# Weight blocks split into high and low halves by transfers instead of by engines, in a two-layer encoder trunk

## The chip, the cores and the metric

The kernel runs on one core of a Trainium2 chip. The metric is the device time of one execution, in microseconds (us). Profiles are of one execution, on the same core.

The engines are named as the profile names them: PE is TensorE (PEld its weight loads), DVE is VectorE, ACT is ScalarE, POOL is GpSimd, SP is SyncE. An engine works through its own instructions in order. A transfer is issued by one of these engines; its data then move by the 16 DMA engines.

## The reference

Two layers (DEPTH 2) of a bidirectional encoder over 512 tokens of width 1024, all in float32:

```python
x = layer_norm(x, ln_in_g, ln_in_b)
for l in range(2):
    proj = x @ w_in[l]                            # 1024 x 6816, split into q, k, v, latents, gates
    na_out  = neighbourhood_attention(...)        # 8 heads of 64, windows of 8 x 16 tokens
    df_out  = diff_attention(...)                 # 4 heads, two softmaxes each
    mla_out = latent_attention(...)               # 8 heads, low-rank q and kv, w_mla_qb, w_mla_kvb
    gates = sigmoid(gate_pre + b_gate[l])         # 3 x 1024 channels
    merged = sum of gates[b] * (branch_b @ w_branch[l, b])
    x = layer_norm(ALPHA * x + merged @ w_out[l])
    gu = x @ w_ffn_in[l]                          # 1024 x 5632
    x = layer_norm(ALPHA * x + (silu(gu[:, :2816]) * gu[:, 2816:]) @ w_ffn_out[l])
```

## The kernel before

PE multiplies in a reduced form of float32 (`float32r`). To keep float32 accuracy each operand is written as a high half (the value rounded to float32r) and a low half (what is left), and each product is made of three matmuls: high x high, high x low, low x high (`mm3`, lines 159 to 161). The activations lie in SBUF in halves as well (`xth`, `xtl` and the slots `r`).

Weights come in blocks of at most 128 x 1024 words. A block holds 2, 3 or 4 row tiles of 128 rows with 512, 336 or 256 columns. `wload` transfers a block from HBM into a tile `raw` (two buffers), issued by SP, and `wsplit` makes the halves: ACT copies `raw` into `whi` (line 141), DVE subtracts `whi` from `raw` into `wlo` (line 142). Both stand in a high-priority scope of the scheduler. `whi` and `wlo` have four buffers each, in rotation; a buffer is free when PE has done the last matmul that reads it. `wload_ks` calls `wload` for a whole product: 4 blocks of 2 x 512 for one half of the output projection (`out_proj`), 3 blocks for one half of one group of the FFN's second product (`ffn_down`), 3 + 3 + 2 row tiles for one half of the latents, two blocks for a gate or a pair of heads, one block for a merge of a branch.

Not by `wload` go the blocks of the first FFN product (`ffn_fast`: seven products of 24 matmuls with 256 columns each, whose blocks are sums and differences made on DVE and split by `wsplit`, in the same four buffers), the latent attention's own weights (`wload_flat`) and the first FFN step of a layer (`wload_slots`).

In a layer the order of the work is: the values of neighbourhood attention (`na_values`), `latents`, then the mixers (4 head pairs, 4 latent pairs, 4 differential heads) with the gates and merges placed between them by the table `PLAN`, then `out_proj`, and then the FFN, in which the halves of `ffn_down` for the group before stand between the steps of `ffn_fast`. The framework's scheduler sets each engine's order at build time from its own estimates of durations, so a change of one helper moves instructions throughout the program.

POOL does little: the small powers of the norms (`rpow`, lines 234 and 235) and a part of each layer norm.

## Time and profile before

| | |
|---|---|
| time, median of 2 runs | 1873.42 us (1872.22 to 1874.62) |
| the profiled execution's own time | 1868.85 us |
| its span, first to last instruction | 1867.1 us |
| PE busy | 1818.0 us, 11200 matmuls |
| DVE, ACT, POOL busy | 1324.6, 915.3, 134.9 us |
| data moved by DMA | 195.88 MB, mean 105 GB/s |

Times of rows are us from the span's start, or durations. A row of the groups gives line, engine, operation, out<-in, shapes, count, then busy us and mean ns of one, then how long the engine had been idle before these instructions and what ended that. A row of the timeline gives start, length, engine, line and operation, then the idle time before it and what ended it. PE's matmuls overlap in the records, so the pace of PE is the distance of their starts.

### The profile page before, as it was taken

Reading aid. Unit: us, or ns where it says so; the run is one execution under the profiler, and the core shown is the slowest. Engines: PE = TensorE matmul, PEld = TensorE weight load, DVE = VectorE, ACT = ScalarE, POOL = GpSimd, SP = SyncE. Lnnn points to the kernel's source line nnn. Section 1 sums busy time; section 2 is a strip of 40 time slices with the busy share of each in tenths; the row PEclk is TensorE's granted clock in tenths of the full one; section 3 lists DMA queues with packets and bytes.
Section 4 is the critical chain, followed back from the end, with each engine's and each line's share of the span. In section 5 each row is a group of like instructions: output and inputs, shape, how many; then the busy total and the mean of one; then the engine's idle time right before and its main releaser. Section 6 shows DMA issues by size and latency. Waiting matters only on the chain.

```text
span 1867.1 us, 28608 instructions
## 1 busy us (share of the span) xinstructions
PE 1818.0 (97%) x11200; PEld 1622.1 (87%) x11200; DVE 1324.6 (71%) x2198; ACT 915.3 (49%) x1629; POOL 134.9 (7%) x217
## 2 busy tenths in 40 slices
PE   7999999999999999999999999999999989999997
PEld 5988899988878999999779888999888789999995
DVE  6488887665568877777546888866655689776766
ACT  3567776555433443333236677755554245333330
POOL 4100000000004000000031000000000120000001
PEclk9999999999999999999999999999999999999999
DMA  7453232222261232323355432322233413323231
GB/s 255 115 163 94 89 91 85 74 85 74 91 212 37 78 115 89 115 89 104 105 156 156 123 97 86 91 62 86 74 101 120 158 46 103 112 91 113 91 102 68
DMA packets 167767, 195.88 MB, mean 105 GB/s; under 512 B 8528, under 2 KB 132688, under 8 KB 167632
## 3 DMA queue, kind: packets, MB, share of 16 engines
q1 hardware_dynamic: 167632, 194.05, 33.4%
q8 instruction: 88, 1.44, 0.3%
q14 instruction: 47, 0.39, 0.1%
HBM read 177.24 MB, written 9.44 MB: 100 GB/s over the span
## 4 chain that ended last, share of the span: by engine, by line
PE 87%; DVE 4%; DMA 3%; POOL 2%; ACT 2%; issue 1%; SPq 0%; POOLq 0%; DVEq 0%; ACTq 0%
PE acc L159 17%; PE acc L160 17%; PE acc L161 17%; PE sc L780 11%; PE pv L780 8%; DVE wlo L142 2%; PE tr L650 2%; PE pv L493 1%; DMA raw<-in_w_ffn_in_dram 1%; DMA f<-in_w_ffn_in_dram 1%; PE sc L479 1%; PE pv L658 1%; PE pv L657 1%; ACT whi L141 1%; PE sc L634 1%
## 5 line engine op out<-in xcount | busy, mean ns | idle before, releaser
L141 ACT ACTIVATE whi<-raw 128x1024 fp32r<-128x1024 f32 (+4 forms) x246 | 254.2, 1034 | 261.6 <-PE acc L160 49.4
L142 DVE TENSOR_TENSOR wlo<-raw,whi 128x1024 fp32r<-128x1024 f32 (+4 forms) x246 | 292.9, 1192 | 126.2 <-ACT whi L141 122.9
L159 PE MATMUL acc<-xth,whi 128*128 128x512 f32 x512 | 203.9, 398 | 0.2 <-ACT f L674 0.2
L161 PE MATMUL acc<-xth,wlo 128*128 128x512 f32 x512 | 202.7, 396 | 0.0
L160 PE MATMUL acc<-xtl,whi 128*128 128x512 f32 x512 | 202.6, 396 | 0.0
L159 PE MATMUL acc<-whi,r 128*128 128x512 f32 (+1 forms) x504 | 194.2, 392 | 4.3 <-DVE f L713 2.2
L141 ACT ACTIVATE whi<-f 128x1024 fp32r<-128x1024 f32 x100 | 104.7, 1056 | 188.8 <-PE acc L161 84.1
L161 PE MATMUL acc<-whi,r 128*128 128x512 f32 (+1 forms) x504 | 197.1, 391 | 0.0
L160 PE MATMUL acc<-wlo,r 128*128 128x512 f32 (+1 forms) x504 | 196.9, 391 | 0.0
L159 PE MATMUL acc<-whi,xth 128*128 128x256 f32 (+2 forms) x576 | 175.2, 306 | 3.0 <-ACT whi L141 2.2
L160 PE MATMUL acc<-wlo,xth 128*128 128x256 f32 (+2 forms) x576 | 175.6, 305 | 1.3 <-DVE wlo L142 1.3
L161 PE MATMUL acc<-whi,xtl 128*128 128x256 f32 (+2 forms) x576 | 175.8, 306 | 0.0
L780 PE MATMUL pv<-r,whi 128*128 128x256 f32 x960 | 173.9, 280 | 1.4 <-DVE P L848 1.4
L780 PEld LDWEIGHTS pv<-r,whi 128*128 128x128 f32 x960 | 148.0, 188 | 3.2 <-issue 2.1
L142 DVE TENSOR_TENSOR wlo<-f,whi 128x1024 fp32r<-128x1024 f32 x100 | 121.8, 1227 | 30.7 <-ACT whi L141 30.6
L780 PE MATMUL sc<-xth,whi 128*128 128x256 f32 x480 | 135.9, 283 | 0.0
L780 PE MATMUL sc<-xtl,whi 128*128 128x256 f32 x480 | 135.3, 282 | 0.0
L780 PE MATMUL sc<-xth,wlo 128*128 128x256 f32 x480 | 134.9, 282 | 0.0
L780 PE MATMUL pv<-r,wlo 128*128 128x256 f32 x480 | 134.0, 279 | 0.0
L234 POOL TENSOR_SCALAR ring<-ring 128x1 f32<-128x1 f32 x68 | 27.4, 404 | 1412.8 <-ACT otmp L499 811.1
L159 PEld LDWEIGHTS acc<-whi,r 128*128 128x128 f32 x504 | 94.2, 188 | 26.1 <-DVE f L713 3.1
L159 PEld LDWEIGHTS acc<-whi,xth 128*128 128x128 f32 x576 | 109.2, 190 | 8.0 <-ACT whi L141 2.9
(225 smaller groups left out, 4351.0 us busy)
## 6 DMA issues: line engine op xcount, KB each, us to landing
raw<-in_w_in_dram SPq DMA_DIRECT2D x64, 512.0 KB, 3.6
f<-in_w_ffn_in_dram SPq DMA_DIRECT2D x60, 512.0 KB, 3.5
raw<-in_w_ffn_out_dram SPq DMA_DIRECT2D x44, 512.0 KB, 3.6
raw<-in_w_in_dram SPq DMA_DIRECT2D x64, 256.0 KB, 3.3
raw<-in_w_ffn_in_dram SPq DMA_DIRECT2D x28, 512.0 KB, 3.6
raw<-in_w_branch_dram SPq DMA_DIRECT2D x24, 512.0 KB, 3.4
raw<-in_w_out_dram SPq DMA_DIRECT2D x16, 512.0 KB, 3.6
r<-r SPq DMA_DIRECT2D x56, 128.0 KB, 2.8
```

The lines of the kernel that those rows point to most:

```text
L141: A.activation(hi[:, :n], raw[:, :n], AF.Copy)
L142: V.tensor_sub(lo[:, :n], raw[:, :n], f32(hi[:, :n]))
L159: T.matmul(o, lh[0], rh[0], start=first, stop=False)
L160: T.matmul(o, lh[0], rh[1], start=False, stop=False)
L161: T.matmul(o, lh[1], rh[0], start=False, stop=last)
L234: G.tensor_scalar(dst, src, eps, None, op0=OP.add)
L479: T.matmul(sc, qs[j][:, tsl(t)], ks[j][1], start=False, stop=True)
L493: T.matmul(po[:, 0:256], ch_[:, tsl(k)], v, start=k == 0, stop=False)
L634: T.matmul(sc, q[0][:, tsl(t)], k[1], start=False, stop=False)
L650: T.transpose(pt[:, tsl(i)], prs[i % 2][:, tsl(kp + i // 2)], ident)
L657: T.matmul(oc, v, ph[:, c], start=kt == 0, stop=False)
L780: T.matmul(o[:, c], w[a][:, j, f], x[e], start=fresh and mi == 0 and j == 0 and n == 0, stop=j == 3 and n == 2, skip_group_check=True)
```

## The change

`wload` no longer uses `raw`, SP or DVE. POOL issues a transfer from HBM straight into `whi`; since the target is float32r and the source float32, it casts. ACT then writes the negated high half into `wlo`. A second transfer, issued by POOL too, reads the same words from HBM again and adds them onto `wlo` in place. A block of two segments (a query and a key slice) takes two transfers for each half. There is no high-priority scope in the new `wload`. `wsplit` is as before for its other callers.

```diff
     def wload(segs, nk, ncol):
-        raw = wp.tile([128, 1024], F32, tag="raw", name="raw", bufs=2)
-        rv = raw[:, :nk * ncol].rearrange("p (k c) -> p k c", k=nk)
+        hi = wp.tile([128, 1024], F32R, tag="whi", name="whi")
+        lo = wp.tile([128, 1024], F32R, tag="wlo", name="wlo")
+        hi, lo = (i[:, :nk * ncol].rearrange("p (k c) -> p k c", k=nk) for i in (hi, lo))
         c = 0
         for src in segs:
             w = src.shape[1]
-            nc.sync.dma_start(rv[:, :, c:c + w], src.rearrange("(k p) c -> p k c", p=128))
+            nc.gpsimd.dma_start(hi[:, :, c:c + w], src.rearrange("(k p) c -> p k c", p=128))
             c += w
-        hi, lo = wsplit(raw, nk * ncol)
-        return hi.rearrange("p (k c) -> p k c", k=nk), lo.rearrange("p (k c) -> p k c", k=nk)
+        A.activation(lo, f32(hi), AF.Copy, scale=-1.0)
+        c = 0
+        for src in segs:
+            w = src.shape[1]
+            nc.gpsimd.dma_start(lo[:, :, c:c + w], src.rearrange("(k p) c -> p k c", p=128), accum_op=OP.add)
+            c += w
+        return hi, lo
```

In all, 196 blocks go by `wload`. SP issues 228 transfers fewer (517 before, 289 now), POOL issues 456 (none before), DVE does 196 subtractions fewer (346 before, 150 now), ACT does as many instructions as before. In the changed program the lines below `wload` stand 6 lines further down; its cast transfer is L133, its negation L135, its accumulating transfer L139.

First place: the end of `na_values` and the two halves of `latents` in layer 1, on ACT. Before, the rows of `whi<-raw` are the high halves, and L523 takes PE's results away:

```order
L141 ACTIVATE whi<-raw 128x1008 x2
L224 ACTIVATE r_80<-acc 128x2x2x64
L141 ACTIVATE whi<-raw 128x672
L224 ACTIVATE r_81<-acc 128x2x2x64
L141 ACTIVATE whi<-raw 128x1008
L523 ACTIVATE f_118<-acc 128x336
L523 ACTIVATE f_119<-acc 128x336
L523 ACTIVATE f_112<-acc 128x336
```

Now, on POOL (the first three casts are the first half's blocks, the fourth and the two 336-column casts behind the accumulating rows are the second half's, 4 x 128 are the two segments of the first head pair's first block):

```order
L133 DMA whi<-in_w_in_dram 128x3x336 x2
L133 DMA whi<-in_w_in_dram 128x2x336
L133 DMA whi<-in_w_in_dram 128x3x336
L139 DMA wlo<-in_w_in_dram 128x3x336 x2
L139 DMA wlo<-in_w_in_dram 128x2x336
L139 DMA wlo<-in_w_in_dram 128x3x336
L133 DMA whi<-in_w_in_dram 128x3x336
L133 DMA whi<-in_w_in_dram 128x2x336
L133 DMA whi<-in_w_in_dram 128x4x128 x2
L139 DMA wlo<-in_w_in_dram 128x3x336
L139 DMA wlo<-in_w_in_dram 128x2x336
L139 DMA wlo<-in_w_in_dram 128x4x128 x2
```

Four cast transfers stand ahead of the first accumulating one: the first block's low half is issued behind the cast of the fourth block, which waits for the fourth buffer.

Second place: `out_proj` in layer 1. Before, SP issues the eight blocks, with other loads between them:

```order
L132 DMA raw<-in_w_branch_dram 128x4x256 x4
L132 DMA raw<-in_w_out_dram 128x2x512
L887 DMA fp_9077<-in_feat_dram 128x30
L132 DMA raw<-in_w_out_dram 128x2x512 x2
L962 DMA f_117<-xd_123 128x1024
L132 DMA raw<-in_w_out_dram 128x2x512
```

Now on POOL, from the last merges on:

```order
L133 DMA whi<-in_w_branch_dram 128x4x256 x2
L139 DMA wlo<-in_w_branch_dram 128x4x256 x2
L133 DMA whi<-in_w_out_dram 128x2x512
L139 DMA wlo<-in_w_out_dram 128x2x512
L133 DMA whi<-in_w_out_dram 128x2x512 x2
L139 DMA wlo<-in_w_out_dram 128x2x512 x2
L133 DMA whi<-in_w_out_dram 128x2x512
L139 DMA wlo<-in_w_out_dram 128x2x512
L133 DMA whi<-in_w_out_dram 128x2x512 x4
L139 DMA wlo<-in_w_out_dram 128x2x512 x4
```

The second half's four casts stand ahead of its first accumulating transfer.

Third place: `ffn_down`. Before, SP issues its blocks into `raw` between those of `ffn_fast` (L822); now POOL issues them, three blocks for each half of a group:

```order
L133 DMA whi<-in_w_ffn_out_dram 128x2x512 x2
L139 DMA wlo<-in_w_ffn_out_dram 128x2x512
L133 DMA whi<-in_w_ffn_out_dram 128x2x512
L139 DMA wlo<-in_w_ffn_out_dram 128x2x512 x2
L133 DMA whi<-in_w_ffn_out_dram 128x2x512 x3
L139 DMA wlo<-in_w_ffn_out_dram 128x2x512 x3
```

In four of the six groups of a layer the third cast stands between the first and second accumulating transfer, in one (the last two rows here) all three casts stand first.

## The prediction

> **What bounds the kernel now.** First the page's head, then what PE waits for, then PE's pace, then the chain by which a weight block becomes ready.

> ```profile
> span 1867.1 us, 28608 instructions
> PE 1818.0 (97%) x11200; PEld 1622.1 (87%) x11200; DVE 1324.6 (71%) x2198; ACT 915.3 (49%) x1629; POOL 134.9 (7%) x217
> PE 87%; DVE 4%; DMA 3%; POOL 2%; ACT 2%; issue 1%; SPq 0%; POOLq 0%; DVEq 0%; ACTq 0%
> ...
> PE tr L266 <- DVE f L256: 9.7, 1, 9.7
> ...
> PE acc L159 <- ACT whi L141: 2.2, 2, 1.6
> ...
> PE acc L160 <- DVE wlo L142: 1.3, 2, 0.8
> ```

> PE is busy for 97% of the span, and the chain that ended last lies on PE for 87%. Its longest wait, 9.7 us, is the start. For the halves of weight blocks it waits 3.5 us in all (2.2 + 1.3). So what the change takes off DVE hardly shortens anything; what matters is whether blocks still arrive before PE wants them.

> ```profile
> 549.51 0.39 PE L159 MATMUL acc<-whi,r 128*128 128x512 f32 x1
> 549.75 0.39 PE L160 MATMUL acc<-wlo,r 128*128 128x512 f32 x1
> ...
> 599.79 0.28 PE L159 MATMUL pv<-xth,r 128*128 128x256 f32 x1
> 599.91 0.28 PE L160 MATMUL pv<-xtl,r 128*128 128x256 f32 x1
> ...
> 47.05 0.32 PE L159 MATMUL acc<-whi,xth 128*128 128x336 f32 x1
> 47.21 0.31 PE L160 MATMUL acc<-wlo,xth 128*128 128x336 f32 x1
> ```

> The starts give PE's pace: 0.233 us for 512 columns, 0.12 for 256, 0.155 for 336. With it, the order of matmuls can be counted in time: from the matmul that frees a buffer to the first that needs the next block's low half in it. I call this the lead. A block that takes longer than its lead stops PE.

> Before, little has to happen within the lead, because `raw` is loaded ahead. This is the second half of `out_proj`:

> ```profile
> 546.26 1.06 ACT L141 ACTIVATE whi<-raw 128x1024 fp32r<-128x1024 f32 x1 [5.91 <-PE acc L161]
> ...
> 547.35 1.23 DVE L142 TENSOR_TENSOR wlo<-raw,whi 128x1024 fp32r<-128x1024 f32 x1 [1.12 <-ACT whi L141]
> ...
> 552.40 1.06 ACT L141 ACTIVATE whi<-raw 128x1024 fp32r<-128x1024 f32 x1 [3.68 <-DMA raw<-in_w_out_dram]
> ```

> PE frees a buffer, ACT starts at 546.26, and DVE ends at 548.58: 2.3 us. The third block, for which `raw` had to be loaded anew, already waits 3.68 us for its transfer.

> **The change, step by step.** Removed: 196 subtractions of DVE at 1.2 us (row below), some 234 us on an engine for which PE waits 1.3 us. I count -3.5 us, all PE waits on L141 and L142. ACT's work stays: a copy becomes a negation of the same size.

> ```profile
> L141 ACT ACTIVATE whi<-raw 128x1024 fp32r<-128x1024 f32 (+4 forms) x246 | 254.2, 1034 | 261.6 <-PE acc L160 49.4
> L142 DVE TENSOR_TENSOR wlo<-raw,whi 128x1024 fp32r<-128x1024 f32 (+4 forms) x246 | 292.9, 1192 | 126.2 <-ACT whi L141 122.9
> ...
> 503.90 0.37 SPq L132 DMA_DIRECT2D raw<-in_w_out_dram  x1
> L251 POOL TENSOR_TENSOR f<-f,f 128x512 f32<-128x512 f32 x16 | 22.4, 1405 | 8.3 <-ACT f L250 8.1
> ...
> raw<-in_w_in_dram SPq DMA_DIRECT2D x64, 512.0 KB, 3.6
> f<-xd SPq DMA_DIRECT2D x8, 512.0 KB, 4.4
> f<-in_x_dram SPq DMA_DIRECT2D x4, 512.0 KB, 8.4
> q1 hardware_dynamic: 167632, 194.05, 33.4%
> ```

> Added, all behind the freed buffer: an issue on POOL, a landing, the negation, a second issue, a second landing. No row shows a transfer from POOL, a casting one or an accumulating one, so each has bounds:
> - Issue: SP takes 0.37 us; POOL takes 1.4 us for an operation on 128x512. I take 1.2, nearer POOL's own row, and as upper end 2.8, twice POOL's row, for a transfer with 512 runs instead of 256.
> - Cast landing after the issue: 3.6 - 0.37, about 3.3; upper end 8.4, the slowest row of 512 KB.
> - Negation: 1.06 us and the hand-overs, 1.4 (lower end 1.1).
> - Accumulating landing: it reads its target too, so I take the slower row, 4.5; lower end 3.2, upper end 8.4.

> The chain is 1.2 + 3.3 + 1.4 + 1.2 + 4.5 = 11.6 us (8.2 to 22) where it was 2.3. Where POOL's order puts the accumulating transfer behind the cast of a later block, the tail after that later buffer is freed counts instead: two issues and a landing, 1.2 + 1.2 + 4.5 = 6.9 us (3.9 to 14).

> [...]

> By place, for one layer (leads counted in matmuls of the changed order):
> - *Latents.* The first half's first accumulation stands behind the fourth cast, whose buffer comes free only as this half begins: 6.9 less 2 matmuls, 6.6. In the second half the lead of the second block is 35 matmuls of 0.155, 5.4 us: 11.6 - 5.4 = 6.2. The next head pair's second block loses 4.4: two cast issues of the next gate stand ahead of its accumulations. Sum 17.2.
> - *out_proj.* The fourth block of the first half has 39 matmuls of 0.233, 9.1 us: 2.5. The second half's first accumulation stands behind the fourth cast, free as the half begins: 6.9 - 0.5 = 6.4. Sum 8.9.
> - *ffn_down.* The first blocks of the six halves have leads of 9.1, 8.6, 6.7, 8.0 and 9.1 us, and one stands behind three casts (3.3): 2.5 + 3.0 + 4.9 + 3.6 + 2.5 + 3.3 = 19.8. The last group, with nothing of `ffn_fast` beside it, has 6.8 and then 6.1 behind two casts: 4.8 + 5.5. Sum 30.1.
> - *Mixers.* A two-segment block needs two issues more, 14.0 us, and its second block waits behind them; leads are 13.8 to 17.4 us. I take 1.5 us for each of 8 groups, 12, and four single blocks with leads of 8.6 to 10.9 give 7.6. Sum 19.6.

> A layer loses 75.8 us, two lose 151.6. At the start four cast issues and a landing under load put the first low half about 5 us later. Then POOL's queue: `rpow` now stands behind transfers that wait for ACT or PE.

> ```profile
> DVE ost L501 <- POOL ring L235: 19.6, 20, 1.4
> L235 POOL TENSOR_TENSOR ring<-ring,expo 128x1 f32<-128x1 f32 x68 | 44.6, 656 | 5.2
> ```

> DVE waits for it at the end of each query tile of a differential head, 20 times up to 1.4 us, and behind that wait stand the next softmax steps. I add 1 us for each of 32 such steps: 32 (none at best, 4 us each at worst).

> Sum: -3.5 + 151.6 + 5 + 32 = 185 us. The profiled execution's own time is 1868.85, so 2054; it lies 0.2% below the median of the runs shown, which I neglect. With every lower end, a layer loses 17 us (latents 7.4, out_proj 3.4, ffn_down 6.2): 1901. With every upper end it loses some 320: over 2500. The second reading of the weights adds about 100 MB to 194, and a share of 33.4% becomes some 50 to 67%: no bound by itself, but a reason for longer landings.

> [...]

> **Rivals.**
> 1. *The order covers it: not slower.* The scheduler has left 9 to 12 us for most blocks of `ffn_down` and 14 and more in the mixers. If the chain takes no more than about 8.5 us, only the tails behind later casts remain: 1901, within 2%. It decides at issues of 0.4 us and plain landings. For it: the 2.3 to 3.6 us of plain rows. Against: a second landing cannot overlap the first. Faster by 2% would need 37 us of PE's idle time back, of which block waits are 3.5.
> 2. *Accumulation is slow.* Landings of 7 us instead of 4.5 add 2.5 us at about 25 places a layer: +125, 2180. For it: DMA load, and a target that is read and written. Against: 3.6 us for 512 KB leaves little that scales with bytes.
> 3. *POOL is the bound in the mixers.* If a 512-run transfer costs 2.8 us to issue, a head pair's two blocks take 8 x 2.8 + 4.7 + 4.5 = 31.6 us against leads near 15: 16 us for each of 8 groups; gates, 4 x 2.8 + 9.2 = 20.4, lose 3 at 14 places; the four short ones 5 each. That is 190 a layer instead of 20, 2390 at most; as a late block lengthens the next lead too, 2300. For it: even one column takes POOL 0.66 us (L235). Against: 7% busy before.

> **How the numbers follow.** My forecast, 1980 to 2130, has 0.5; rival 2 (2130 to 2230) 0.17; rival 3 (2230 to 2330, and 0.06 beyond) 0.21; rival 1 0.08, 0.02 of it faster; between 1911 and 1980 0.04. Beyond 2% (what a measurement can tell from no change) is 1911 upward: slower 0.92, same 0.06. The range 1940 to 2330 leaves out rival 1 and the slowest cases.

> **What would show it.** PE's waits should name DMA `wlo` at L165 to L167, 2 to 7 us each, some 50 to 70 of them; POOL's issues about 1.2 us; `wlo` landings near 4.5; DVE some 235 us less busy, and that without effect. At the second half of `out_proj` PE should stand 6 us once a layer. If PE shows no such waits, the chain is short and rival 1 holds; if POOL is busy in the mixers, rival 3. I am wrong altogether if the time falls below 1911.

## The result and the profile after

The changed kernel took 2205.78 us (median; 2203.78 to 2207.77) against 1873.42 us: a ratio of 1.178, with a 95% interval of 1.175 to 1.182. The forecast was 2054 us, in a range of 1940 to 2330.

First the head of the page of the changed kernel: span, busy time, the two DMA queues (POOL's transfers are `software_dynamic`), and the transfers with their median time from the start of the issue to the landing.

```profile
span 2201.9 us, 28837 instructions
PE 1919.2 (87%) x11200; PEld 1679.7 (76%) x11200; DVE 1111.6 (50%) x2002; ACT 907.7 (41%) x1629; POOL 586.5 (27%) x673
q0 software_dynamic: 199808, 201.88, 50.7%
q1 hardware_dynamic: 67728, 93.11, 13.5%
whi<-in_w_in_dram POOLq DMA_DIRECT2D x64, 512.0 KB, 5.0
wlo<-in_w_in_dram POOLq DMA_DIRECT2D x64, 512.0 KB, 6.1
f<-in_w_ffn_in_dram SPq DMA_DIRECT2D x60, 512.0 KB, 3.5
whi<-in_w_ffn_out_dram POOLq DMA_DIRECT2D x44, 512.0 KB, 5.3
wlo<-in_w_ffn_out_dram POOLq DMA_DIRECT2D x44, 512.0 KB, 6.9
```

The span grew by 334.8 us (2201.9 - 1867.1). It splits in two: PE is *busy* for 101.2 us more (1919.2 - 1818.0) with the same 11200 matmuls, and *idle* for 233.6 us more (282.7 instead of 49.1). An idle part of 185 us was forecast, a busy part was not. DVE lost 213 us of work, and nothing came of it. SyncE's plain transfers still land in 3.5 us; POOL's in these rows take 5.0 to 6.9.

What PE waits for, by line, in the changed kernel (us in total, times, longest):

```profile
PE acc L166 <- DMA wlo<-in_w_ffn_out_dram: 70.4, 23, 6.4
PE acc L166 <- DMA wlo<-in_w_out_dram: 35.8, 8, 8.4
PE acc L166 <- DMA wlo<-in_w_in_dram: 35.2, 11, 6.2
PE acc L167 <- DMA wlo<-in_w_in_dram: 13.2, 7, 3.3
...
PE acc L167 <- DMA wlo<-in_w_branch_dram: 12.0, 4, 4.6
```

These are 53 waits and 166.6 us, all for the accumulating transfer; before, both halves together cost 3.5 us. PE's other idle time grew too, from 45.6 to 116.1 us, and the largest part of that are waits for ScalarE and VectorE (32.9 us before, 77.3 now). One of the 53 waits, for the fourth block in the first half of `out_proj`, in order of time (start, duration, instruction, and in brackets the idle time before it):

```profile
620.60 1.22 POOL L133 DMA_DIRECT2D whi<-in_w_out_dram  x1
...
631.79 1.06 ACT L135 ACTIVATE wlo<-whi 128x1024 fp32r<-128x1024 f32 x1 [9.30 <-DMA whi<-in_w_out_dram]
...
633.14 1.19 POOL L139 DMA_DIRECT2D wlo<-in_w_out_dram  x1 [11.32 <-ACT wlo L135]
...
638.89 0.80 PE L166 MATMUL acc<-wlo,r 128*128 128x512 f32 x1 [4.67 <-DMA wlo<-in_w_out_dram]
639.48 0.63 PE L167 MATMUL acc<-whi,r 128*128 128x512 f32 x1
639.91 0.63 PE L165 MATMUL acc<-whi,r 128*128 128x512 f32 x1
...
644.04 0.39 PE L167 MATMUL acc<-whi,r 128*128 128x512 f32 x1
644.27 0.39 PE L165 MATMUL acc<-whi,r 128*128 128x512 f32 x1
```

The whole chain is there: cast issued at 620.60, landed by 631.79, negated, accumulating transfer issued at 633.14 and landed by 638.89, 18.3 us in all. It is a long one: the cast, issued right behind the accumulating transfer of the block before (which landed after 9.7 us), took 11.1 us. At the second half, where the prediction put 6 us, PE stands still for 8.4:

```profile
664.62 0.79 PE L166 MATMUL acc<-wlo,r 128*128 128x512 f32 x1 [8.41 <-DMA wlo<-in_w_out_dram]
```

Behind the stall at 638.89 comes what the prediction did not have: matmuls of 512 columns start 0.43 us apart (639.48 to 639.91), and only from 644 on 0.23 us apart. The windows say why. In this view a line is a stretch, then the busy time of each engine with its instructions, the granted clock of TensorE (1.00 is full speed), the DMA share and GB/s:

```profile
638.80:643.00 4.20, 4.11 (x10) 3.24 (x11) 1.38 (x2) 0.00 (x0) 0.00 (x0) 0.50 0.00 0
643.00:646.00 3.00, 3.00 (x13) 2.40 (x12) 1.38 (x2) 0.00 (x0) 0.00 (x0) 0.86 0.00 0
```

The granted clock is 0.50 for 4 us behind the stall, with no transfer under way. This stall is thus paid for twice. Over the whole run the trace's clock records show 0.5 for 246.0 us (30.6 before); PE was busy in 175.5 of them (19.5 before), and half of that is counted as lost, 78.0 us more than before. The other 23.2 us of the busy part go with the number of stops, 123 waits of PE instead of 20: with 512 columns the last matmul before a stop lasts 0.39 us where the next would otherwise start after 0.23, and behind a stop the first two starts are 0.34 us apart instead of 0.23 (in the serial run below), together some 0.27 us, or 28 us for 103 stops. This is an estimate.

Layer 1 by stages, from the first to the last matmul of 336 columns (latents), to the first and the last of `ffn_fast`, and to the next layer's latents; first before, then after, then (see the experiments) with a second transfer that doesn't add:

```profile
42.20:73.30 31.10, 30.02 (x193) 29.50 (x192) 10.90 (x28) 12.93 (x28) 5.59 (x12) 1.00 0.42 117
73.30:602.70 529.40, 524.94 (x3075) 458.90 (x3075) 380.94 (x747) 304.20 (x616) 37.78 (x61) 1.00 0.34 102
602.70:891.30 288.60, 284.48 (x2042) 267.20 (x2041) 216.59 (x244) 116.11 (x138) 0.41 (x2) 0.99 0.31 99
891.30:966.40 75.10, 69.09 (x299) 54.93 (x298) 45.64 (x69) 24.07 (x34) 19.58 (x26) 0.95 0.39 124
```

```profile
54.10:102.80 48.70, 35.07 (x191) 34.18 (x192) 4.79 (x22) 13.22 (x28) 18.98 (x24) 0.82 0.70 126
102.80:717.90 615.10, 554.24 (x3075) 474.58 (x3074) 310.14 (x683) 302.47 (x617) 198.80 (x221) 0.96 0.74 143
717.90:1040.70 322.80, 295.22 (x2042) 273.78 (x2041) 198.80 (x227) 115.03 (x137) 32.50 (x35) 0.96 0.44 112
1040.70:1144.00 103.30, 76.27 (x300) 58.34 (x298) 32.78 (x58) 23.23 (x34) 38.90 (x49) 0.87 0.67 152
```

```profile
52.90:97.60 44.70, 34.14 (x191) 33.25 (x192) 4.79 (x22) 13.19 (x28) 14.77 (x24) 0.85 0.61 137
97.60:665.10 567.50, 537.89 (x3075) 464.67 (x3074) 310.76 (x684) 303.12 (x618) 153.36 (x221) 0.98 0.67 155
665.10:972.20 307.10, 290.14 (x2042) 270.32 (x2041) 198.01 (x225) 114.74 (x137) 23.67 (x35) 0.98 0.39 118
972.20:1068.20 96.00, 75.73 (x300) 57.63 (x298) 32.76 (x58) 23.38 (x34) 34.92 (x50) 0.91 0.58 163
```

The largest part of the loss is in the mixers with `out_proj` (the second stretch of each: 529.4, then 615.1), and there PE's own busy time went from 524.9 to 554.2 us for the same matmuls, at a mean clock of 0.96.

### The profile page after: what moved, and what is told of

Its sections match the earlier page's. It is cut to its first block, busy times and chain, and to the rows that moved or that the text cites. A ratio compares the mean times of both kernels' runs of the same rounds, so it can differ in the third digit from the quotient of the medians.

```text
span 2201.9 us, 28837 instructions
## 1 busy us (share of the span) xinstructions
PE 1919.2 (87%) x11200; PEld 1679.7 (76%) x11200; DVE 1111.6 (50%) x2002; ACT 907.7 (41%) x1629; POOL 586.5 (27%) x673
## 2 busy tenths in 40 slices
DMA packets 267672, 296.83 MB, mean 135 GB/s; under 512 B 12176, under 2 KB 215184, under 8 KB 267536
## 3 DMA queue, kind: packets, MB, share of 16 engines
q1 hardware_dynamic: 67728, 93.11, 13.5%
## 5 line engine op out<-in xcount | busy, mean ns | idle before, releaser
L135 ACT ACTIVATE wlo<-whi 128x1024 fp32r<-128x1024 f32 (+3 forms) x196 | 203.9, 1043 | 471.4 <-DMA whi<-in_w_in_dram 167.6
L166 PE MATMUL acc<-wlo,r 128*128 128x512 f32 (+1 forms) x504 | 217.5, 432 | 106.2 <-DMA wlo<-in_w_ffn_out_dram 70.4
L139 POOL DMA_DIRECT2D wlo<-in_w_in_dram x140 | 185.4, 1516 | 248.9 <-ACT wlo L135 184.1
L165 PE MATMUL acc<-whi,r 128*128 128x512 f32 (+1 forms) x504 | 208.4, 420 | 17.4 <-ACT f L577 8.9
L167 PE MATMUL acc<-xth,wlo 128*128 128x512 f32 x512 | 207.0, 404 | 13.2 <-DMA wlo<-in_w_in_dram 13.2
L167 PE MATMUL acc<-whi,r 128*128 128x512 f32 (+1 forms) x504 | 213.1, 423 | 0.0
L166 PEld LDWEIGHTS acc<-wlo,r 128*128 128x128 f32 x504 | 105.4, 209 | 138.2 <-DMA wlo<-in_w_ffn_out_dram 76.5
L165 PE MATMUL acc<-xth,whi 128*128 128x512 f32 x512 | 207.0, 404 | 3.0 <-issue 2.8
L133 POOL DMA_DIRECT2D whi<-in_w_in_dram x140 | 125.4, 1010 | 272.2 <-PE acc L167 179.9
L165 PE MATMUL acc<-whi,xth 128*128 128x256 f32 (+2 forms) x576 | 181.8, 316 | 10.8 <-DVE r L231 5.7
L167 PE MATMUL acc<-whi,xtl 128*128 128x256 f32 (+2 forms) x576 | 180.2, 313 | 0.0
L133 POOL DMA_DIRECT2D whi<-in_w_ffn_out_dram x44 | 37.2, 869 | 527.9 <-PE pv L786 281.2
L166 PEld LDWEIGHTS acc<-wlo,xth 128*128 128x128 f32 x576 | 113.9, 198 | 42.2 <-DMA wlo<-in_w_in_dram 28.0
L165 PEld LDWEIGHTS acc<-whi,r 128*128 128x128 f32 x504 | 103.5, 208 | 44.8 <-ACT f L577 9.4
## 6 DMA issues: line engine op xcount, KB each, us to landing
whi<-in_w_in_dram POOLq DMA_DIRECT2D x64, 512.0 KB, 5.0
wlo<-in_w_in_dram POOLq DMA_DIRECT2D x64, 512.0 KB, 6.1
f<-in_w_ffn_in_dram SPq DMA_DIRECT2D x60, 512.0 KB, 3.5
whi<-in_w_ffn_out_dram POOLq DMA_DIRECT2D x44, 512.0 KB, 5.3
wlo<-in_w_ffn_out_dram POOLq DMA_DIRECT2D x44, 512.0 KB, 6.9
raw<-in_w_ffn_in_dram SPq DMA_DIRECT2D x28, 512.0 KB, 3.5
```

Source lines behind the costliest of these rows:

```text
L133: nc.gpsimd.dma_start(hi[:, :, c:c + w], src.rearrange("(k p) c -> p k c", p=128))
L135: A.activation(lo, f32(hi), AF.Copy, scale=-1.0)
L139: nc.gpsimd.dma_start(lo[:, :, c:c + w], src.rearrange("(k p) c -> p k c", p=128), accum_op=OP.add)
L165: T.matmul(o, lh[0], rh[0], start=first, stop=False)
L166: T.matmul(o, lh[0], rh[1], start=False, stop=False)
L167: T.matmul(o, lh[1], rh[0], start=False, stop=last)
```

## Experiments

Theory A: a block's low half comes out of a chain of serial steps, longer than the time until PE wants it, and each stall is followed by some microseconds at half clock. Its rivals: B, instructions that stand in order behind waiting ones on ScalarE and POOL carry the loss; C, the doubled reading loads the DMA engines. The results in one table (us; PE idle is span less busy time, and "more" is against the kernel before). Half clock is half of the time that PE was busy at a granted clock of 0.5; it is a part of the busy time. The chain is the median over the 228 transfers of a run, from the start of a cast's issue to the landing of the same block's second transfer.

| kernel | time | ratio (95% interval) | PE idle more | PE busy more | half clock more | chain |
|---|---|---|---|---|---|---|
| changed kernel | 2205.78 | 1.178 (1.175 to 1.182) | 233.6 | 101.2 | 78.0 | 13.9 |
| no second transfer | 1902.72 | 1.016 (1.012 to 1.020) | 19.5 | 10.7 | 1.5 | |
| cast alone | 1932.33 | 1.032 (1.029 to 1.035) | 41.9 | 20.7 | 8.8 | |
| accumulation alone | 2076.78 | 1.109 (1.106 to 1.112) | 143.1 | 66.4 | 51.6 | |
| before, one raw buffer | 2006.60 | 1.072 (1.069 to 1.075) | 92.2 | 46.4 | 23.6 | |
| second transfer plain | 2058.65 | 1.100 (1.095 to 1.104) | 128.0 | 58.6 | 44.1 | 10.9 |
| no wait for the cast | 2026.85 | 1.083 (1.078 to 1.087) | 103.9 | 50.5 | 31.4 | 9.9 |
| negation on VectorE | 2202.14 | 1.176 (1.172 to 1.181) | 234.0 | 102.5 | 82.4 | 13.7 |
| five high buffers | 2065.77 | 1.103 (1.099 to 1.108) | 135.2 | 59.7 | 42.7 | 15.8 |
| raw by POOL | 1885.29 | 1.006 (1.004 to 1.008) | 14.3 | 2.5 | 0.4 | |

**No second transfer.**

```diff
         A.activation(lo, f32(hi), AF.Copy, scale=-1.0)
-        c = 0
-        for src in segs:
-            w = src.shape[1]
-            nc.gpsimd.dma_start(lo[:, :, c:c + w], ..., accum_op=OP.add)
-            c += w
         return hi, lo
```

> The accumulating transfer is left out, so the low half is the bare negated high half and the product is not the reference's; the casting transfer, the negation and every matmul stay. Theory A (the loss is the length of the chain that a block runs through once its buffers are free, about 13.7 us in the changed kernel: issue and cast landing 1.0 + 5.2, negation 1.3, issue and accumulate landing 1.4 + 5 to 7; and the half clock of TensorE behind each stall): the chain is cut to about 7.5 us, most of the 254 us of TensorE gaps go, and the clock's mean goes back towards 0.985: 1890 to 1920 us. Theory B (queues in program order: negations on ScalarE that wait for a cast landing hold up the softmax and normalisation behind them, transfers on POOL hold up its powers): the negations and the casts are still there, so the stages of mixers keep half or more of their 80 us each: 1960 to 2020 us. Theory C (the DMA engines are loaded by the second reading): 1890 to 1920 like A, but then landings of the casts fall from 5.2 to about 4 us.

1902.72 us, where A said 1890 to 1920. The casts from POOL and the negations that wait for them are all still there and cost 30 us together. That leaves 303 of the 332 us to the accumulating transfer, and the mixers, which B wanted to stay slow, went from 529.4 to 537.9 us. The casts' landings fell from 5.0 to 4.1 us (512 KB of `w_in`), as C said, so load by the second transfer is real; what it costs by itself this run does not say.

**Cast alone.** Lines against the changed kernel; the tile `raw` is back, `rv` and `hv` are views of `raw` and `hi`, and `n` is the block's width.

```diff
-            nc.gpsimd.dma_start(hi[:, :, c:c + w], ...)
+            nc.sync.dma_start(rv[:, :, c:c + w], ...)
+            nc.gpsimd.dma_start(hv[:, :, c:c + w], ...)
...
-        A.activation(lo, f32(hi), AF.Copy, scale=-1.0)
-        (accumulating transfer)
+        with tc.high_priority():
+            V.tensor_sub(lo[:, :n], raw[:, :n], f32(hi[:, :n]))
```

> The high half still comes by a casting transfer issued on POOL, the raw block comes by SyncE beside it, and VectorE subtracts at high priority as in the kernel before; no negation and no accumulating transfer, same bytes read as in the changed kernel. Theory A (serial chain): the two transfers run side by side, the chain is about 1.0 + 5.2 + 1.1 = 7.3 us, but the high buffer is free only a block late: 1880 to 1930 us. Theory B (queues in order, POOL's share): POOL still issues 220-odd casts, ScalarE holds nothing: 1880 to 1900 if ScalarE's negations are what costs, 1930 to 1980 if POOL's are. Theory C (load of the second reading): the same 390 MB-equivalents of reading as in the changed kernel, so landings stay long and the time is 1950 or more.

1932.33 us, 2 above A's upper end; C (1950 or more) fails. This kernel moves the same 296.83 MB as the changed one (no row has the 390 of the expectation), through the same 16 DMA engines, in 273 us less: reading the weights twice is not what costs here, where the two readings go side by side.

**Accumulation alone.** Lines against the changed kernel, with `raw` back as above.

```diff
-            nc.gpsimd.dma_start(hi[:, :, c:c + w], ...)
+            nc.sync.dma_start(rv[:, :, c:c + w], ...)
...
+        with tc.high_priority():
+            A.activation(hi[:, :n], raw[:, :n], AF.Copy)
+            A.activation(lo[:, :n], f32(hi[:, :n]), AF.Copy, scale=-1.0)
             (accumulating transfer as in the changed kernel)
```

> The raw block comes by SyncE and is copied to the high half by ScalarE as in the kernel before; ScalarE then negates it, and the low half is made by the accumulating transfer issued on POOL. Theory A: the chain from the free buffer is ScalarE's copy 1.1, negation 1.3, issue 1.4, accumulate landing 5 to 7, about 9 to 11 us against 13.7, since the raw block is fetched ahead: 1950 to 2040 us, gaps of TensorE about half of the changed kernel's. Theory B: ScalarE carries two passes for a block but waits for prefetched data alone, so the mixers recover more than the feed-forward part: 1930 to 1970 us. Theory C: same bytes, so landings as in the changed kernel, 6 us or more for the accumulating one: 2050 or more.

2076.78 us: above A's 2040 and inside C's range. The row shows where A was too low:

```profile
wlo<-in_w_ffn_out_dram POOLq DMA_DIRECT2D x44, 512.0 KB, 8.9
```

With raw blocks fetched ahead at the same time, the accumulating landing rose from 6.9 to 8.9 us. Alone it took 5.8 us for 512 KB of `w_in` (in the serial run below). So beside other transfers it lands later: C has a share, through the length of the chain.

**Before, one raw buffer.**

```diff
-        raw = wp.tile([128, 1024], F32, tag="raw", name="raw", bufs=2)
+        raw = wp.tile([128, 1024], F32, tag="raw", name="raw", bufs=1)
```

> The kernel before with one raw buffer in place of two, so that a block's transfer starts only when the block ahead has been split: stalls of TensorE without any transfer on POOL. A block then takes landing 3.5 plus issue and split about 2.3, some 6 us against 5.6 us of matmuls a block where blocks follow closely, so the time should be 1880 to 1960 us. Theory A's part on the clock: whatever idle time TensorE gains, the time of its matmuls grows too, by about 0.35 us for each 1 us of new gaps (in the changed kernel 79 us of slower matmuls for 228 us of new gaps). The rival (the slow matmuls of the changed kernel come from its transfers, memory writes beside TensorE's reads for example, not from stalls): the matmuls stay within 5 us of the time they take in the kernel before, whatever the gaps.

2006.6 us, 47 above the upper end; where that comes from was not followed up (the mixers of layer 1 alone took 568.5 us). Its purpose was the clock: no transfer from POOL, no accumulation, and the matmuls slow down all the same.

```profile
PE 1864.4 (93%) x11200; PEld 1634.9 (82%) x11200; DVE 1331.3 (66%) x2198; ACT 915.4 (46%) x1629; POOL 128.7 (6%) x217
```

PE is busy 46.4 us longer and idle 92.2 us longer. By the clock records 23.6 of the 46.4 us are half clock, 0.26 us for each microsecond of new idle time (0.33 in the changed kernel, 78.0 for 233.6); the expectation said about 0.35. The rival (the transfers slow the matmuls, and without them they stay within 5 us) fails. In the table the half clock costs 0.26 to 0.36 us for each microsecond of new idle time in the seven kernels that stall for 90 us more or longer, and less where the stalls are few: 0.21 with the cast alone, 0.08 without a second transfer. All of the longer busy time together, stops included, is 0.43 to 0.55.

**Second transfer plain.** The low half is then a copy of the high half.

```diff
-            nc.gpsimd.dma_start(lo[:, :, c:c + w], ..., accum_op=OP.add)
+            nc.gpsimd.dma_start(lo[:, :, c:c + w], ...)
```

> The second transfer casts and overwrites the negated high half in place of adding onto it, so the low half is a copy of the high half and the product is not the reference's. Bytes read from memory, queue, number of instructions and the chain of waits are those of the changed kernel; only the reading back and adding at the destination is gone. Leaving the second transfer out altogether gave 1902.7 us, so 303 us are to be divided. Theory A1 (the addition itself makes the landing long): the second landing falls from 6 to 7 us to 4 to 5 us, the chain from 13.7 to about 11.5 us, 2050 to 2120 us. Theory A2 (any second transfer behind the first in series costs it, the addition nothing): 2170 to 2210 us. Theory C (second reading loads the DMA engines): 2170 or more, like A2, but then the first landing stays at 5 us and above as well.

2058.65 us: A1. Same waits, queue, bytes and order as the changed kernel (every engine's instructions stand in the same order), but the second transfer lands as fast as any:

```profile
whi<-in_w_ffn_out_dram POOLq DMA_DIRECT2D x44, 512.0 KB, 5.2
wlo<-in_w_ffn_out_dram POOLq DMA_DIRECT2D x44, 512.0 KB, 4.6
```

Added in this order, the 332 us divide into 30 (casts from POOL and negation), 156 (a second transfer in series) and 147 (that it adds at its target). The last is 3.0 us of chain (13.9 against 10.9): by medians of all blocks the second landing is 1.9 us shorter (4.1 against 6.0, issue included) and the cast's 0.7 (4.6 against 5.3).

**No wait for the cast.** The low half is then the whole weight; `l8` is `lo` in eight parts and `zero` a small tile of zeros.

```diff
-        A.activation(lo, f32(hi), AF.Copy, scale=-1.0)
+        A.activation(l8, zero[:, :m // 8].unsqueeze(1).to_broadcast([128, 8, m // 8]), AF.Copy, scale=-1.0)
```

> ScalarE fills the low half with zeros (same engine, size of the pass and number of passes) in place of the negated high half, so its pass and the accumulating transfer no longer wait for the cast to land; the low half is then the whole weight and the product is not the reference's. Transfers, bytes and additions are those of the changed kernel. Theory A (length of the chain): a block is ready after about 1.0 fill + 1.4 issue + 6.5 landing = 9 us from a free buffer in place of 13.7 us, and ScalarE no longer waits for a landing: 1980 to 2060 us. Theory C (load of the accumulating transfers on the DMA engines, which here overlap the casts more): accumulating landings rise to 8 to 10 us and the time stays at 2100 to 2200 us. Theory B (ScalarE and POOL held up by waits in their queues): the mixers come back to within 20 us of the kernel before, and the feed-forward part stays where it was.

2026.85 us, inside A's range, 179 below the changed kernel with every transfer and addition still there. C's other half came true too: the two transfers now overlap more (for `ffn_out` the cast takes 7.9 us and the accumulating one 9.2, and the median chain is 9.9), which may be why no more is won. B's own forecast fails: the mixers are at 568.8 us (39 over the kernel before), and the feed-forward part did come back, from 322.8 to 300.9. But the edit changed more than the chain. The scheduler placed the transfers anew, so that 189 of the 228 accumulating ones have no later block's cast ahead of them on POOL (93 in the changed kernel), and PE's waits for ScalarE and VectorE fell from 77.3 to 41.4 us (36.4 in the kernel before). The 179 us belong to the chain and to the queues together.

**Negation on VectorE.**

```diff
-        A.activation(lo, f32(hi), AF.Copy, scale=-1.0)
+        V.tensor_scalar(lo, f32(hi), -1.0, None, op0=OP.mult)
```

> The negation runs on VectorE in place of ScalarE; nothing else differs from the changed kernel. Theory A (length of the chain): the pass takes about as long there, the chain stays near 13.5 us: 2180 to 2230 us. Theory B (ScalarE's instructions stand behind a negation that waits for a cast to land, and PE waits for them): ScalarE is free and VectorE, half idle, takes the waits: mixers win back 20 to 40 us of their 80 a layer, 2110 to 2170 us; if VectorE's queue is the one that matters more, the time rises over 2240 us.

2202.14 us, the changed kernel's time; neither of B's forecasts came. What PE waits for did change: for ScalarE 17.6 us instead of 38.2, for VectorE 58.3 instead of 39.1. So a waiting negation holds up what stands behind it, whichever engine does it. In the changed kernel it looks like this, where the merges end:

```profile
603.07 1.06 ACT L135 ACTIVATE wlo<-whi 128x1024 fp32r<-128x1024 f32 x1 [7.77 <-DMA whi<-in_w_out_dram]
604.03 0.61 ACT L233 ACTIVATE r<-f 128x512 fp32r<-128x512 f32 x1
...
604.68 0.69 DVE L234 SCALAR_TENSOR_TENSOR r<-f,r 128x512 fp32r<-128x512 f32 x1 [7.31 <-ACT r L233]
...
605.28 0.68 DVE L693 SCALAR_TENSOR_TENSOR f<-f,acc 128x512 f32<-128x512 f32 x1
...
606.02 0.58 PE L165 MATMUL acc<-r,whi 128*128 128x512 f32 x1 [4.61 <-DVE f L693]
```

ScalarE stands still for 7.77 us until a cast has landed and it can negate that block; the split of a merge (L233) stands behind the negation, VectorE waits for the split, and PE for VectorE. So B has a share: by the traces at most the 44 us by which PE's waits for ScalarE and VectorE grew, and what half clock follows them. It needs the long landings of A, for without a second transfer these waits are 47.6 us (36.4 before).

**Parts measured by themselves, first try.** Transfers of each kind, then bursts of 60 matmuls behind idle times made by a chain on VectorE.

> Not the kernel's computation: transfers of a weight block one after the other with nothing else running (plain by SyncE, plain by POOL, casting by POOL, then negation and accumulating transfer), in the shapes 2x512, 4x256, 4x128 in two parts and 4x128 in one; then bursts of 60 matmuls behind idle times of TensorE from about 1 to 11 us. Theory A: a plain 512 KB block lands in about 3.5 us by either queue, the cast in about 4, the accumulating one in 5.5 to 7 even alone; theory C (contention makes the landings long): alone the accumulating one lands in 4 to 4.5. On the clock: if a stall itself slows what follows, the matmuls of a burst take 1.25 to 1.35 times 232 ns for 3 to 5 us behind an idle time of 3 us or more, and less or nothing behind 1 us; if transfers slow them, bursts here run at full speed from the start.

The transfers told nothing, since the three kinds ran beside each other (5.8 to 8.9 us for 512 KB of all of them). The bursts were clear: behind idle times of 6.3 us and more, also where no transfer was left, each began at 427 ns a matmul for about 3 to 6 us and then ran at 227 ns.

**Parts measured by themselves, in series.** All kinds through one buffer (`one` in the code), so that each waits for the last; idle times made by a chain on ScalarE.

> Not the kernel's computation: the transfers of a weight block strictly one behind the other through one buffer (in the earlier measurement the three kinds ran beside each other, so their landings of 5 to 9 us were under load); then bursts of 60 matmuls behind idle times of TensorE from about 0.6 to 5 us. Theory A (the addition itself makes the landing long): plain by SyncE about 3.5 us, plain by POOL and casting about 4, accumulating 5.5 or more for 512 KB. Theory C (load makes it long): accumulating 4 to 4.5 us. On the clock: the bursts behind 6 us and more began at 427 ns a matmul for 2.6 to 5.3 us, then 227. If any stall does this, the bursts behind 0.6 us do it too; if the stall has to fill a window, those behind less than about 3 us run at 227 ns from the start or only some of them are slow.

Median times from the start of the issue to the landing, alone:

```profile
sp<-in_w_in_dram SPq DMA_DIRECT2D x10, 512.0 KB, 3.4
pool<-in_w_in_dram POOLq DMA_DIRECT2D x10, 512.0 KB, 3.9
cast<-in_w_in_dram POOLq DMA_DIRECT2D x10, 512.0 KB, 3.9
lo<-in_w_in_dram POOLq DMA_DIRECT2D x10, 512.0 KB, 5.8
```

Here, with nothing else under way, going by POOL costs 0.5 us (3.9 against 3.4), casting nothing, adding 1.9 us (5.8 against 3.9). A's figure is met (5.5 or more), C's (4 to 4.5) is not. The expectations above counted the issue twice beside these landings; the rows hold it already. The clock, one row for each burst with its duration and the idle time before it:

```profile
408.40 13.89 PE L164 MATMUL acc<-mv,lh 128*128 128x512 f32 x60 [0.71 <-ACT lh L161]
...
470.39 13.89 PE L164 MATMUL acc<-mv,lh 128*128 128x512 f32 x60 [2.07 <-ACT lh L161]
486.76 15.52 PE L164 MATMUL acc<-mv,lh 128*128 128x512 f32 x60 [2.47 <-ACT lh L161]
505.38 16.55 PE L164 MATMUL acc<-mv,lh 128*128 128x512 f32 x60 [3.09 <-ACT lh L161]
...
626.09 15.51 PE L164 MATMUL acc<-mv,lh 128*128 128x512 f32 x60 [2.07 <-ACT lh L161]
```

Behind 0.4 to 1.8 us of idle time a burst takes 13.9 us, behind 2.47 us and more 1.6 to 2.8 us longer, and 2.07 us gave the one and the other. The clock records go with this: in this run the granted clock changes only at steps of 3.41 us, and it falls behind steps in which PE stood still long enough. Two such steps (the stalls of 2.07 and 3.09 us begin in them), each with the next:

```profile
466.74:470.15 3.41, 1.58 (x7) 0.96 (x6) 0.00 (x0) 1.63 (x6) 0.00 (x0) 1.00 0.00 0
470.15:473.56 3.41, 3.17 (x14) 2.63 (x15) 0.00 (x0) 0.19 (x1) 0.00 (x0) 1.00 0.00 0
...
500.87:504.28 3.41, 1.41 (x7) 0.83 (x5) 0.00 (x0) 1.80 (x6) 0.00 (x0) 1.00 0.00 0
504.29:507.69 3.40, 2.31 (x6) 1.83 (x7) 0.00 (x0) 0.94 (x4) 0.00 (x0) 0.50 0.00 0
```

PE is idle for 1.83 us of the first step and keeps its clock; it is idle for 2.00 us of the other, and the next step is granted 0.50. In this run none of the steps at full clock with 1.83 us or less lost it and every one with 2.00 or more did; in the changed kernel steps with up to 1.77 us kept it, and the least that lost it was 1.60 us. In the changed kernel PE stands still for 2.5 us or more 37 times, in the kernel before 5 times (the wait at the start left out).

**Five high buffers.** The `whi` line stands in `wload` and in `wsplit`, the `raw` line in three other places.

```diff
-        hi = wp.tile([128, 1024], F32R, tag="whi", name="whi")
+        hi = wp.tile([128, 1024], F32R, tag="whi", name="whi", bufs=5)
...
-        raw = wp.tile([128, 1024], F32, tag="raw", name="raw", bufs=2)
+        raw = wp.tile([128, 1024], F32, tag="raw", name="raw", bufs=1)
```

> Five buffers for high halves in place of four (one raw buffer in place of two makes the room), so a cast can land a block ahead; the accumulating transfer still needs one of four low buffers. Theory A (length of the chain from the freed buffer): negation 1.1, issue 1.4 and landing 6.5 are left of 13.7 us, about 9 us: 2040 to 2120 us, some of it taken back by the single raw buffer in the feed-forward part. Theory B (order on POOL): accumulating transfers now stand behind more casts that wait for a buffer on the same queue (two casts ahead at 127 of the 228, where it was one at 93 and two at 91), so the gain is given back: 2150 to 2230 us.

2065.77 us, so A, though the chain from cast to landing got longer (15.8 us): it starts a block earlier. What counts is the chain *against* the time a block has. B's order on POOL fails here as the cause: more accumulating transfers than in the changed kernel have a later block's cast ahead of them (207 of 228, against 135), and the time is 140 us shorter.

**Raw by POOL.**

```diff
-            nc.sync.dma_start(rv[:, :, c:c + w], src.rearrange("(k p) c -> p k c", p=128))
+            nc.gpsimd.dma_start(rv[:, :, c:c + w], src.rearrange("(k p) c -> p k c", p=128))
```

> The kernel before with its raw weight blocks issued on POOL in place of SyncE, nothing else: plain transfers, fetched one block ahead, split by ScalarE and VectorE. It prices POOL's queue by itself: issues of 0.8 to 1.4 us, and powers of the normalisations that stand behind transfers which wait for a buffer. The prediction put 32 us on that. Theory A (chain length only): 1872 to 1885 us. Theory B (POOL's queue matters): 1900 to 1930 us, with VectorE's waits for POOL in the mixers 20 to 40 us longer than in the kernel before.

1885.29 us, the upper edge of A's range and well under B's. VectorE's wait for POOL's powers at the end of the query tiles:

```profile
DVE ost L501 <- POOL ring L235: 24.6, 26, 1.8
```

That is 5 us more than the 19.6 of the kernel before, not 32.

## Why the prediction held, and where it did not

**PE is the bound and DVE's relief is worth nothing: right.** DVE's 213 us bought no time (with the negation on VectorE it works 123 us more, in the same time), and PE's waits name the accumulating transfer, 53 of them of 0.3 to 8.4 us (50 to 70 of 2 to 7 us forecast).

**What the missing 152 us are.** The time lies in the stated range, but above the 1980 to 2130 us that had 0.5. PE's waits for low halves were put at 151.6 us and came to 166.6: 15 us. The half clock, 78 us, and the stops' 23 us were not in the sum. Other idle time grew by 70.5 us where the start and `rpow` had 37: 33 us. The last 2 us are the median above the profiled execution.

**The chain, 11.6 us: right alone, too short under load.** In series and alone it took 11.0 us (median): 3.9 for issue and cast, 1.4 to the second issue, 5.6 to 5.8 for issue and accumulation (forecast 4.5, 1.4 and 5.7). In the kernel it took 13.9 us: the casts of 256 and 512 KB land in 4.6 to 6.6 us and the accumulating transfers in 5.8 to 7.5 (medians; the four blocks of `w_mlv` are quicker, 3.1 and 5.0). The prediction noted that double reading is "a reason for longer landings", and put nothing for it into the sum. Rival 2 (landings of 7 us, +125, 2180) named the landings and the band in which the time lies, but not the way there: its 125 us were waits for low halves, and these are only 15 us over the sum. That the transfer adds is worth 147 us all the same, 76 of them in these waits (166.6 against 90.4 with a plain second transfer). The prediction put the accumulating landing above the cast's because it reads its target too. It was longer, by 1.9 us for 512 KB alone (5.8 against 3.9); that reading the target is the reason was the author's assumption, and no run separates the reading from the add. Two bounds do not come out of their terms: the listed upper ends of the chain add up to 23.8 us, not 22, and the lower ends give 1899 us, not 1901. The forecast hangs on neither.

**The half clock: missing from the sum.** It is the term that failed outright: the sum prices a stall at its length, and 78 us of half clock behind the stalls came on top. By the clock records of the serial run, 2.00 us of idle time within one step of 3.41 us were enough for it, and it lasted one or two such steps there.

**By places, layer 1.** The sum's terms against the stretches above, and PE's waits for low halves within them:

| place | forecast | changed: longer | waits | second plain: longer | waits |
|---|---|---|---|---|---|
| latents | 17.2 | 17.6 | 11.3 | 13.6 | 8.2 |
| mixers, `out_proj`, and half of `rpow`'s 32 | 19.6 + 8.9 + 16 = 44.5 | 85.7 | 36.1 | 38.1 | 18.2 |
| `ffn_down` beside `ffn_fast` | 19.8 | 34.2 | 19.0 | 18.5 | 8.9 |
| last group, to the next latents | 10.3 | 28.2 | 19.3 | 20.9 | 12.5 |
| sum | 91.8 | 165.7 | 85.7 | 91.1 | 47.8 |

The waits of the changed kernel, 85.7 us, are close to the 75.8 of the sum without `rpow`. That was in part luck: it took a chain of 13.9 us, and with 10.9 us they are 47.8, so for its own 11.6 the sum had them too high. In the same way the run with a chain of 10.9 us comes out almost as forecast for 11.6 because 58.6 us of longer busy time fill up what is missing: idle time was 128 us there, not 185.

The largest miss is the second row. The mixers' own blocks are not its cause: PE waited 14.7 us for their low halves (19.6 forecast) and 3.3 us for the next head pair's, which the prediction counted with the latents. `out_proj` has 18.0 us where 8.9 were forecast, 9.6 for 2.5 in its first half and 8.4 for 6.4 in its second. PE's waits for ScalarE, VectorE and POOL in this stretch went from 4.4 to 21.6 us, and its busy time grew by 29.3.

**`rpow` behind POOL's transfers, +32: too large at the wait that it names.** In the changed kernel VectorE's wait at the query tiles is 37.0 us against 19.6, 17 us more; with the other waits for the powers it is 66.5 against 31.1. Raw blocks through POOL cost 12 us in all, and there VectorE waited 5 us longer at the query tiles. How much of this reaches PE is not shown.

**Issues of 1.2 us: about right.** POOL needs 0.72 to 0.77 us for a cast and 1.2 to 1.3 for an accumulating transfer (medians); the upper figures are for 512 runs, the lower for 256, so twice the runs cost 0.03 to 0.11 us. Rival 3 (2.8 us) did not come, nor rival 1: the median landings of 4.6 to 7.5 us are longer than SyncE's 3.5, and the order does not cover the chain.

**Start, +5: too small.** The first latents came 11.9 us later.

Nothing tried beats the kernel before, and no result points to one that would: its block waits are 3.5 us. The casts' landings grow with the additions for `w_in` (512 KB: 3.9 us alone, 4.1 without a second transfer, 4.2 with a plain one, 5.0 in the changed kernel), but for `w_ffn_out` they are 4.9 us already without a second transfer and 5.3 with it. What stays open is how the loss divides between the chain and the instructions held up behind it: no run takes away the one and leaves the other as it was.

## What to carry to other kernels

Two transfers in series where there was one fetched ahead cost the time by which the whole chain exceeds the lead of a block, so compare chain and lead under the new load, and give the chain a buffer's lead before counting what it saves elsewhere. In this kernel, bound by TensorE, each microsecond of new idle time brought 0.43 to 0.55 us of longer busy time in the nine runs with 19 us of it and more, so it cost 1.43 to 1.55 times its length; in the seven with 90 us and more, 0.26 to 0.36 of that was half clock. Look for the same in the clock records of your own traces before you price a stall at its length. A pass that waits for a transfer holds up whatever stands behind it on its engine: here ScalarE stood still for 7.77 us before a negation, and PE for 4.61 us behind it. An engine that the bound engine does not wait for is no place to look for time: 213 us off VectorE bought nothing.
